# Gaps of 64 and 32 bytes in the pool of slots of a two-block network on one core

## The chip, the core and the metric

The program runs on one core of one Trainium2 chip, batch 1, 256 tokens of 1,024 features. The metric is the device time of one execution in microseconds (us). The kernel before was timed in 2 runs: 2258.93 and 2261.82 us, median 2260.38 us. One more execution was profiled; the rows below are from it.

## What is computed

Two blocks of two layers each, in float32, one behind the other on the same 256 tokens. Nearly all of the arithmetic is products of the tokens with weights that are read once from HBM (the reference, cut):

```python
def first_block(x, ...):                      # layers 0 and 1
    for layer in range(2):
        h = h + 0.5 * _swiglu(_rmsnorm(h, norm_ffn1[layer]), wg, wu, wd)   # 1024 -> 2816 -> 1024
        hn = _rmsnorm(h, norm_mix[layer])
        h = h + (_attn_conv_mixer(hn, ...) if layer == 0 else _recurrent_mixer(hn, ...))
        h = h + 0.5 * _swiglu(_rmsnorm(h, norm_ffn2[layer]), wg, wu, wd)
    return _rmsnorm(h, norm_final)

def second_block(x, c, positions, ...):       # layers 0 and 1
    for layer in range(2):
        sh1, sc1, g1, sh2, sc2, g2 = split(silu(c) @ ada_w[layer] + ada_b[layer], 6)
        x = x + g1 * _mixer(_rms_norm(x, norm_mix) * (1 + sc1) + sh1, ...)   # three kinds of attention
        h = _rms_norm(x, norm_ffn) * (1 + sc2) + sh2
        y = _swiglu_2(h, ...) if layer == 0 else _moe(h, ...)                # 8 experts, 2 per token
        x = x + g2 * y
    return x
```

## The kernel before

**The product in three parts.** TensorE multiplies float32r operands here, which keep fewer bits than float32. So each weight and each activation is split in a high part and a low part. ScalarE (ACT) copies the float32 tile into a float32r tile, the high part; VectorE (DVE) subtracts it from the float32 tile, and the difference is the low part. `mm3` (L329) then makes three matmuls for each 128 features: tokens-high by weights-high (L334), tokens-low by weights-high (L335), tokens-high by weights-low (L337). In the mixture of experts the small experts hold high and low part of 64 tokens side by side in one operand, and two matmuls do (`prod`, L429). In `fmajor` (L595) the roles are exchanged: the weights are loaded into the array and the tokens stream through it.

A matmul has two operands in SBUF. One is loaded into the array ahead of the matmul, 128 columns of 4 bytes from each partition (`lhsT`; the profile shows the load as LDWEIGHTS on the line PEld). The other streams through the array, mostly 512 columns (`rhs`). In `mm3` the tokens are the operand that is loaded and the weights the one that streams. While one matmul streams, the operand of the next is loaded.

**Where the operands lie.** Weights arrive by DMA in 4 buffers `raw` of 8,192 bytes per partition; their high and low parts go to 8 tiles `wh` and 8 tiles `wl` of 4,096 bytes. Everything of the tokens lies in the pool `slots` (L200): 12 places `s0` to `s11`, of 8,192 bytes (`s8` of 4,096), each used for many things in turn. The normed and transposed tokens `xT` are `s0` (high) and `s1` (low), from `new_xT` (L417); the hidden activations of a feed-forward are `s2` and `s3`; a gathered expert's tokens are `s0` or `s1`. Where slots are free for a while, they serve as additional tiles of weights (`ext`, L312): `s9` and `s10` in most feed-forwards, `s2` in the dense one of the second block. Behind the slots stands the pool `cst` (the residual `x`, the identity matrix, constants), and behind it `sm`, the small tiles.

The pools stand one behind the other in the order in which they are opened, and in `slots` a place is given where its tag is first used. In the built program `raw` begins at byte 16,512 of each partition, `wh` at 49,280, `wl` at 82,048, `slots` at 114,816, `x` at 209,024, `ident` at 217,216. Each of these is a multiple of 128, and so is each slice of 128 or 512 columns of them. So before the change, in every one of the 9,076 float32r matmuls that stream 256 columns or more, the operand that is loaded and the one that streams begin at the same place modulo 128. [...]

**Order.** SP issues the loads of weights in the order in which they are used, each as soon as a `raw` buffer is free. The order on each engine is that of the code. Stages: the feed-forwards and mixers of the first block, then those of the second up to about 1430 us, and from there the mixture of experts.

Of the kernel before, what the change touches and what calls it, by code (L numbers as in the profile page):

```python
# [8 lines left out]
F32 = mybir.dt.float32  # L9
F32R = mybir.dt.float32r  # L10
# [182 lines left out]
class K:  # L193
    def __init__(self, ctx, tc, A, out, dbg=None):
        self.tc, self.nc, self.A, self.out, self.dbg = tc, tc.nc, A, out, dbg or {}
        e = ctx.enter_context
        self.raw_p = e(tc.tile_pool(name="raw", bufs=4))
        self.h_p = e(tc.tile_pool(name="wh", bufs=8))
        self.l_p = e(tc.tile_pool(name="wl", bufs=8))
        self.slots = e(tc.tile_pool(name="slots", bufs=1))  # L200
        self.cst = e(tc.tile_pool(name="cst", bufs=1))
        self.sm_p = e(tc.tile_pool(name="sm", bufs=1))
        self.ps = e(tc.tile_pool(name="ps", bufs=4, space=bass.MemoryType.PSUM))
        self.dr = e(tc.tile_pool(name="dr", bufs=1, space=bass.MemoryType.DRAM))
        self.n = 0
        self.ext, self.turn, self.in_moe, self.c_row = (), 0, False, None
        self.first, self.behind = True, None
        self.setup()
# [206 lines left out]
            self.split_T(xT, t, xn, groups=(g,))  # L415

    def new_xT(self):  # L417
        return (self.slot(0, [128, 2, 8, 128], F32R), self.slot(1, [128, 2, 8, 128], F32R))


    def prod(self, out, xs, groups, c0, n, first, last, half=False):
# [972 lines left out]
    def moe(self, h, res, xT, defer):  # L1394
# [21 lines left out]
        def sm(tag, n=16):  # L1416
            return self.small(tag, n, bufs=1).rearrange("p (t e) -> p t e", t=2)
# [78 lines left out]
        def make(got, i, m, half, pcol, gcol):  # L1496

            one, oneT = m[:, 0:256], m[:, 256:512]
            kinds = [(0, half)]
            tables(one, kinds, pcol)  # L1500
            yield
            eT = self.slot(i % 2, [128, 8, 128] if half else [128, 2, 8, 128], F32R)
            got.update(xk=operand(eT, half), half=half, o32=oneT.bitcast(F32))
            yield from gather(one, kinds, [eT], gcol is None)
            got["gs"] = turned(one, oneT, 1, (gcol or (lambda: [gateS[t][:, 0:1] for t in range(2)]))())
# [24 lines left out]
        ct = self.small("ct", 8, bufs=1)  # L1530
# [14 lines left out]
        def by_slot(tag, v, n=8):  # L1545
            r = self.small(tag, 8, bufs=1)
            self.tt(d1, oh, v[:, None, :].to_broadcast([128, 8, 8]), OP.mult)
            nc.vector.tensor_reduce(out=r, in_=d1, axis=AX.X, op=OP.add)
            return r

        eid = by_slot("eid", self.iota8)
# [10 lines left out]
        gateS = [by_slot(f"gateS{t}", gate[:, t]) for t in range(2)]  # L1562

        pov = sm("pov")
        room = self.small("room", 8, bufs=1)
        self.ts(room, place, 1.0, 2.0, OP.is_equal, OP.add)
        self.ts(place, place, 4.5, op0=OP.is_gt)
        self.tt(place, room, place, OP.subtract)
# [14 lines left out]
        def expert(src, got, out, **kw):  # L1583


            def fin(t, acc):
                ye = out()
                for hh in range(2):
                    sl = slice(hh * 512, (hh + 1) * 512)
                    self.stt(ye[:, sl], acc[hh], got["gs"], g2[:, sl], OP.mult, OP.mult)  # L1590

            self.ffn(src, 0, got["xk"], [0], fin, half=got["half"], **kw)
            for _ in scatter([(got["o32"], out())]):
                pass

        def source(s):
            if s == 0:
# [5 lines left out]
        bufs = [self.slot(2, [128, 2, 2, 512], F32R), self.slot(3, [128, 2, 2, 512], F32R), tmp,  # L1603
                {(0, hh): self.mm(512, "acc") for hh in range(2)}]
# [117 lines left out]
        def store():  # L1722
            for t in range(2):
                for hh in range(2):
                    sl = slice(hh * 512, (hh + 1) * 512)
                    (nc.sync if hh == 0 else nc.scalar).dma_start(out=self.out[t * 128:(t + 1) * 128, sl], in_=self.x[t][:, sl])
# [1 line left out]
        store()  # L1728
        flag = nc.values_load(over_i[0:1, 0:1], min_val=0, max_val=256)
        with self.tc.If(flag > 128):  # L1730
            now = self.small("now", 8, bufs=1)
            nc.vector.memset(now, 0.0)
            pc = self.small("pc", 4, bufs=1)
            tmp = sm("ovt")
            hot = self.small("hot", 8, bufs=1)
            with self.tc.For_i(0, 8, 1) as e:
                self.tt(hot, self.iota8, now, OP.is_equal)
                for a, v in ((0, pov), (1, gate)):
                    self.tt(tmp, v, hot[:, None, :].to_broadcast([128, 2, 8]), OP.mult)
                    nc.vector.tensor_reduce(out=pc[:, 2 * a:2 * a + 2], in_=tmp, axis=AX.X, op=OP.add)  # L1740
                self.ts(now, now, 1.0, op0=OP.add)
                src = A["moe"][bass.ds(e, 1)].rearrange("a n -> (a n)")
                m = self.slot(7, [128, 512], F32R)
                got = {}
                for _ in make(got, 0, m, False, [pc[:, t:t + 1] for t in range(2)], lambda: [pc[:, 2 + t:3 + t] for t in range(2)]):
                    pass
                ye = self.slot(10, [128, D])
                expert(src, got, lambda: ye)
            store()
# [122 lines left out]
```

## Time and profile before

| what | value |
|---|---|
| median of 2 runs | 2260.38 us (2258.93 to 2261.82) |
| the profiled execution, its own time | 2259.85 us |
| its span, first to last instruction | 2258.0 us |
| PE busy | 2200.2 us, 97% |
| PEld (loads of the array) busy | 1812.7 us, 80% |
| DVE busy | 1719.0 us, 76% |
| ACT busy | 1336.0 us, 59% |
| mean granted TensorE clock | 0.996 of full speed |

The profiled execution took 1.85 us more than its span and is 0.5 us under the median, so its rows stand for the runs. A matmul's row gives its start and a duration that is modelled: a 512-column matmul is shown with some 390 ns while the next one starts 227 ns after it, since they are pipelined. So PE's busy share tells that it seldom stands still, not how fast it runs; its pace is read from the distance between starts.

### The profile page before, as it was taken

How to read it: one execution, taken by the hardware profiler on the slowest of the kernel's cores; microseconds unless marked ns; L12 is line 12 of the kernel's file. 1: busy time of each engine (PE TensorE's matmuls, PEld its weight loads, DVE VectorE, ACT ScalarE, POOL GpSimd, SP SyncE). 2: the span in 40 equal slices, each digit the busy share in tenths (PEclk: the TensorE clock that was granted, in tenths of full speed). 3: DMA queues.
4: the chain of work that ended last, by engine and by line, in shares of the span. 5: the costliest groups of instructions: out<-in, count | busy, mean ns of one | idle time of the engine just before them, and what ended most of it. 6: DMA issues, size and time to landing. Idle time of an engine off the chain costs nothing.

```text
span 2258.0 us, 29602 instructions
## 1 busy us (share of the span) xinstructions
PE 2200.2 (97%) x10976; PEld 1812.7 (80%) x10976; DVE 1719.0 (76%) x2205; ACT 1336.0 (59%) x1819; POOL 92.9 (4%) x152
## 2 busy tenths in 40 slices
PE   8999999999999999999999999999999999999998
PEld 6888878888888788887888878887788777877777
DVE  6785967658657886675755666889888999889997
ACT  6445554445436744456544475677767776767764
POOL 0001000000000100030000111000000000000000
PEclk9999999999999999999999999999999999999999
DMA  8784258758764587533555442689988888989886
GB/s 339 267 317 163 99 191 318 258 194 311 262 222 159 193 318 264 207 130 131 215 186 183 143 160 108 249 338 336 336 331 326 326 335 320 344 329 347 325 328 242
DMA packets 82263, 572.92 MB, mean 254 GB/s; under 512 B 9373, under 2 KB 9685, under 8 KB 15424
## 3 DMA queue, kind: packets, MB, share of 16 engines
q1 hardware_dynamic: 77616, 556.73, 66.5%
q0 software_dynamic: 3920, 13.12, 1.7%
q8 instruction: 88, 1.44, 0.2%
q10 hardware_dynamic: 576, 1.11, 0.1%
q14 instruction: 63, 0.52, 0.1%
HBM read 569.80 MB, written 1.12 MB: 253 GB/s over the span
## 4 chain that ended last, share of the span: by engine, by line
PE 46%; DVE 5%; ACT 3%; issue 2%; DMA 1%; POOL 1%; ACTq 0%; DVEq 0%; POOLq 0%
PE mm L334 7%; PE mm L335 7%; PE mm L337 7%; PE mm L429 5%; PE acc L335 4%; PE acc L334 4%; PE acc L337 4%; DVE wl L231 3%; PE acc L429 2%; ACT wh L222 2%; PE mm L1579 1%; ACT s L222 1%; DVE s L231 1%; PE mm L595 1%; PE mm L1467 1%
## 5 line engine op out<-in xcount | busy, mean ns | idle before, releaser
L231 DVE TENSOR_TENSOR wl<-raw,wh 128x1024 fp32r<-128x1024 f32 (+1 forms) x908 | 1078.5, 1216 | 272.4 <-ACT wh L222 259.4
L222 ACT ACTIVATE wh<-raw 128x1024 fp32r<-128x1024 f32 (+1 forms) x908 | 921.0, 1052 | 371.4 <-PE mm L335 152.7
L334 PE MATMUL mm<-wh,s 128*128 128x512 f32 (+2 forms) x1384 | 515.9, 378 | 3.2 <-ACT s L222 3.2
L335 PE MATMUL mm<-wh,s 128*128 128x512 f32 (+2 forms) x1384 | 511.1, 374 | 1.0 <-DVE s L231 1.0
L222 ACT ACTIVATE s<-mm 128x512 fp32r<-128x512 f32 (+7 forms) x387 | 200.1, 534 | 346.8 <-PE mm L337 88.3
L337 PE MATMUL mm<-wl,s 128*128 128x512 f32 (+2 forms) x1384 | 396.1, 374 | 0.2
L334 PE MATMUL acc<-wh,s 128*128 128x512 f32 x788 | 312.0, 397 | 4.0 <-ACT s L222 2.1
L335 PE MATMUL acc<-wh,s 128*128 128x512 f32 x788 | 310.5, 394 | 2.2 <-DVE s L231 2.2
L334 PEld LDWEIGHTS mm<-wh,s 128*128 128x128 f32 x1384 | 261.2, 189 | 50.6 <-ACT s L222 4.9
L335 PEld LDWEIGHTS mm<-wh,s 128*128 128x128 f32 x1384 | 261.7, 189 | 47.7 <-DVE s L231 3.3
L337 PEld LDWEIGHTS mm<-wl,s 128*128 128x128 f32 x1384 | 249.5, 189 | 46.4 <-DVE wl L231 1.2
L337 PE MATMUL acc<-wl,s 128*128 128x512 f32 x788 | 251.9, 392 | 0.6 <-DVE wl L231 0.5
L334 PEld LDWEIGHTS acc<-wh,s 128*128 128x128 f32 x788 | 148.6, 189 | 35.5 <-ACT s L222 3.2
L335 PEld LDWEIGHTS acc<-wh,s 128*128 128x128 f32 x788 | 149.0, 189 | 32.4 <-DVE s L231 4.0
L337 PEld LDWEIGHTS acc<-wl,s 128*128 128x128 f32 x788 | 148.1, 189 | 32.5 <-DVE wl L231 2.2
L429 PE MATMUL mm<-wl,s 128*128 128x512 f32 (+1 forms) x384 | 144.1, 382 | 3.2 <-DVE wl L231 3.1
L429 PE MATMUL mm<-wh,s 128*128 128x512 f32 (+1 forms) x384 | 143.3, 381 | 0.0
L231 DVE TENSOR_TENSOR s<-mm,s 128x512 fp32r<-128x512 f32 (+5 forms) x216 | 128.7, 619 | 17.5 <-ACT s L222 16.7
L987 DVE SCALAR_TENSOR_TENSOR raw<-raw,s 128x1024 f32<-128x1024 f32 x96 | 114.2, 1219 | 4.5 <-DMA raw<-in_ada_w 2.6
L231 DVE TENSOR_TENSOR s<-s,mm 128x512 f32<-128x512 f32 (+1 forms) x93 | 59.6, 641 | 46.7 <-PE mm L337 41.1
L222 ACT ACTIVATE s<-raw 128x1024 fp32r<-128x1024 f32 x50 | 52.5, 1061 | 70.8 <-PE mm L337 33.0
L429 PEld LDWEIGHTS mm<-wl,s 128*128 128x128 f32 x384 | 72.5, 189 | 22.5 <-DVE wl L231 9.2
(308 smaller groups left out, 2187.5 us busy)
## 6 DMA issues: line engine op xcount, KB each, us to landing
raw<-in_moe SPq DMA_DIRECT2D x264, 1024.0 KB, 5.6
raw<-in_f SPq DMA_DIRECT2D x132, 1024.0 KB, 5.9
raw<-in_ada_w SPq DMA_DIRECT2D x48, 1024.0 KB, 5.0
raw<-in_dense SPq DMA_DIRECT2D x33, 1024.0 KB, 4.8
raw<-in_w_in SPq DMA_DIRECT2D x12, 1024.0 KB, 4.9
raw<-in_ow_in SPq DMA_DIRECT2D x8, 1024.0 KB, 5.0
raw<-in_w_out SPq DMA_DIRECT2D x8, 1024.0 KB, 6.2
raw<-in_ew_in SPq DMA_DIRECT2D x7, 1024.0 KB, 5.0
```

Source lines behind the costliest of these rows:

```text
L222: return self.nc.scalar.activation(out=out, in_=in_, func=func, **kw)
L231: return self.nc.vector.tensor_tensor(out=out, in0=in0, in1=in1, op=op)
L334: mm(out=out, lhsT=xs[i][0], rhs=ws[i][0], start=first and i == 0, stop=False)
L335: mm(out=out, lhsT=xs[i][1], rhs=ws[i][0], start=False, stop=False)
L337: mm(out=out, lhsT=xs[i][0], rhs=ws[i][1], start=False, stop=last and i == n - 1)
L429: self.nc.tensor.matmul(out=out, lhsT=x[0], rhs=w[j][:, c0:c0 + n], start=first and k == 0 and j == 0, stop=last and k == len(ws) - 1 and ...
L595: mm(out=out, lhsT=a, rhs=b, start=j == 0, stop=j == len(todo) - 1)
L987: self.nc.vector.scalar_tensor_tensor(out=src, in0=src, scalar=1.0, in1=self.c_row, op0=OP.mult, op1=OP.mult, accum_out=p[:, 2 * pc + i:2 ...
L1467: mm(out=p[:, k * w:(k + 1) * w], lhsT=h[t][:, a, kk * 128:(kk + 1) * 128], rhs=one[:, o:o + w], start=t == 0, stop=t == 1)
L1579: mm(out=p, lhsT=o[:, t * 128:(t + 1) * 128], rhs=v[:, sl], start=b == 0, stop=b == len(parts) - 1)
```

## The change

Two tiles that nobody reads or writes are put into the pool of slots: `gap0`, 64 bytes per partition, ahead of all slots, and `gap1`, 32 bytes, behind `s0` and `s1` (taken at the first call of `new_xT` alone, since `first` is true only there). To make room for these 96 bytes, three small tiles of 32 bytes lose tags of their own: `room` now uses the place of `ct`, and, in the part for an overfull expert at the end, `now` that of `ct` and `hot` that of `eid`. That last part is behind a condition and is not entered in the profiled execution.

```diff
@@ -198,6 +198,7 @@
         self.slots = e(tc.tile_pool(name="slots", bufs=1))
+        self.slots.tile([128, 16], F32, tag="gap0", name="gap0")
         self.cst = e(tc.tile_pool(name="cst", bufs=1))
@@ -415,7 +416,10 @@
     def new_xT(self):
-        return (self.slot(0, [128, 2, 8, 128], F32R), self.slot(1, [128, 2, 8, 128], F32R))
+        xT = (self.slot(0, [128, 2, 8, 128], F32R), self.slot(1, [128, 2, 8, 128], F32R))
+        if self.first:
+            self.slots.tile([128, 8], F32, tag="gap1", name="gap1")
+        return xT
@@ -1562,7 +1566,7 @@
-        room = self.small("room", 8, bufs=1)
+        room = self.small("ct", 8, bufs=1)
         self.ts(room, place, 1.0, 2.0, OP.is_equal, OP.add)
@@ -1728,11 +1732,11 @@
-            now = self.small("now", 8, bufs=1)
+            now = self.small("ct", 8, bufs=1)
             nc.vector.memset(now, 0.0)
...
-            hot = self.small("hot", 8, bufs=1)
+            hot = self.small("eid", 8, bufs=1)
```

In the built program of the change the instructions of PE, ACT, POOL and SP are those of before, in the same order, with the same waits; on DVE seven rows name `ct` or `eid` where they named `room`, `now` or `hot`. So nothing is added, removed or moved in time by the program itself. What differs is addresses. Modulo 128 they are:

| tiles | before | change |
|---|---|---|
| `raw`, `wh`, `wl` | 0 | 0 |
| `s8`, `s0`, `s1` (`xT`, gathered tokens) | 0 | 64 |
| `s2` to `s7`, `s9` to `s11` (hidden activations, additional weights, the rest) | 0 | 96 |
| `x`, `ident`, `ones` | 0 | 96 |
| `consts` | 32 | 0 |

## Rows read from the trace of the kernel before

**Rows 1.** Stages: span, busy us (instructions) of PE PEld DVE ACT POOL, clock, DMA, GB/s

```profile
0.00:1430.00 1430.00, 1399.34 (x7172) 1173.67 (x7173) 978.25 (x1388) 741.12 (x1117) 92.30 (x151) 1.00 0.58 213
1430.00:2258.00 828.00, 800.86 (x3805) 639.08 (x3803) 740.73 (x819) 594.85 (x702) 0.64 (x1) 0.99 0.87 325
```

**Rows 2.** The same stages, line L334 alone: PE busy, PEld busy

```profile
0.00:1430.00 1430.00, 646.33 (x1710) 322.21 (x1710) 1.00 0.58 213
1430.00:2258.00 828.00, 262.02 (x686) 129.65 (x686) 0.99 0.87 325
```

**Rows 3.** The second stage, line L429 alone: PE busy, PEld busy

```profile
1430.00:2258.00 828.00, 271.79 (x1120) 197.07 (x1120) 0.99 0.87 325
```

**Rows 4.** The first stage, line L595 alone: PE busy, PEld busy

```profile
0.00:1430.00 1430.00, 94.54 (x768) 93.08 (x768) 1.00 0.58 213
```

**Rows 5.** Timeline of PE, 512 columns: start us, us, engine, line, tiles

```profile
1534.27 0.39 PE L429 MATMUL mm<-wl,s 128*128 128x512 f32 x1
...
1538.81 0.39 PE L429 MATMUL mm<-wl,s 128*128 128x512 f32 x1
...
1539.86 0.39 PE L429 MATMUL mm<-wl,s 128*128 128x512 f32 x1
...
1541.01 0.39 PE L429 MATMUL mm<-wh,s 128*128 128x512 f32 x1
```

**Rows 6.** Timeline of PE, 256 columns

```profile
1310.68 0.64 PE L595 MATMUL mm<-s,wh 128*128 128x256 f32 x4
1311.16 0.40 PE L595 MATMUL mm<-s,wl 128*128 128x256 f32 x2
```

**Rows 7.** Timeline of PE, 512 columns, among the first matmuls of the program

```profile
14.08 0.63 PE L335 MATMUL mm<-wh,s 128*128 128x512 f32 x1
...
15.36 0.71 PE L337 MATMUL mm<-wl,s 128*128 128x512 f32 x2
```

**Rows 8.** Timeline of PE, plain float32, 256 and 128 columns

```profile
272.03 9.67 PE L784 MATMUL acc<-s,s 128*128 128x256 f32 x44
...
47.60 1.03 PE L457 MATMUL mm<-ident,s 128*128 128x128 f32 x8
```

**Rows 9.** Groups of PE by shape: count, busy us, mean ns of one, idle before

```profile
L457 PE MATMUL mm<-ident,s 128*128 128x128 f32 x326 | 46.8, 274 | 0.0
...
L784 PE MATMUL acc<-s,s 128*128 128x256 f32 x62 | 13.9, 380 | 0.0
```

**Rows 10.** Timeline of PE: matmuls around a late load

```profile
2077.19 0.39 PE L429 MATMUL mm<-wl,s 128*128 128x512 f32 x1
2077.41 0.39 PE L429 MATMUL mm<-wh,s 128*128 128x512 f32 x1
2077.64 0.39 PE L429 MATMUL mm<-wl,s 128*128 128x512 f32 x1
...
2114.95 0.40 PE L335 MATMUL acc<-wh,s 128*128 128x512 f32 x1
2115.19 0.62 PE L337 MATMUL acc<-wl,s 128*128 128x512 f32 x2
```

**Rows 11.** Timeline of PEld: the loads in the same places

```profile
2077.19 0.19 PEld L429 LDWEIGHTS mm<-wh,s 128*128 128x128 f32 x1
2077.46 0.19 PEld L429 LDWEIGHTS mm<-wl,s 128*128 128x128 f32 x1
...
2115.00 0.37 PEld L337 LDWEIGHTS acc<-wl,s 128*128 128x128 f32 x2
```

**Rows 12.** Timeline of PE, 416 columns: the first one and the matmul behind them

```profile
962.35 0.35 PE L334 MATMUL mm<-wh,s 128*128 128x416 f32 x1
...
966.87 0.39 PE L334 MATMUL acc<-wh,s 128*128 128x512 f32 x1
```

**Rows 13.** Groups of DVE by shape: count, busy us, mean ns, idle before

```profile
L239 DVE SCALAR_TENSOR_TENSOR s<-s,cols,s 128x256 f32<-128x256 f32 x90 | 39.2, 479 | 0.6
...
L239 DVE SCALAR_TENSOR_TENSOR s<-s,cols,s 128x255 f32<-128x255 f32 x8 | 3.5, 480 | 6.5 <-ACT s L222 6.5
```

## The prediction

> **What bounds the kernel now.** I read the stages first, one up to 1430 us and the mixture of experts behind it. The reader is to see that PE is busy in 1399 of 1430 us and in 801 of 828, at a granted clock of 1.00 and 0.99, the higher of its two levels (2.4 GHz); DVE is next with 68% and 89%, and the DMA moves 213 and 325 GB/s [rows 1]. So the end is set by how fast PE gets through its matmuls: 31 + 27 = 58 us are all that it stands idle.
>
> Next I read PE's pace, from start to start. With 512 columns, 20 matmuls lie between 1534.27 and 1538.81 us: 227.0 ns each [rows 5]. With 256 columns, four lie between 1310.68 and 1311.16: 120 ns [rows 6]. The difference is 107 ns for 256 columns, 0.418 ns per column, one column per cycle at 2.4 GHz. What is left is the same in both: 227 - 214 = 13 ns, 120 - 107 = 13 ns. So each float32r matmul pays 13 ns, some 6% at 512 columns, for something that isn't its columns. This is the only cost that a change of addresses can touch at a size that counts.
>
> Plain float32 pays less. 44 matmuls of 256 columns take 9.67 us [rows 8], the last of which is shown with 0.38 [rows 9]: 9.29/43 = 216 ns. Eight of 128 columns take 1.03, the last with 0.27: 0.76/7 = 109 ns. That is 0.84 ns per column and a rest of 1 to 3 ns. Their operands too begin at 0 modulo 128. And the first matmuls of the program run at half pace: three in 15.36 - 14.08 = 1.28 us, 427 ns for 512 columns [rows 7], 0.834 ns per column, with no rest. So the 13 ns are there only when 4 bytes are read per partition each 0.418 ns. This is what makes a quarrel of two reads, that of the stream and that of the next operand, possible at all.
>
> **The change part by part.** The program adds, removes and moves no instruction, so every term is a change of durations.
>
> *The float32r matmuls.* There are three lines with 1710 in the first stage and 686 in the second [rows 2], 1120 on L429 [rows 3] and 768 on L595 [rows 4]: 3 x 1710 + 768 = 5898, 3 x 686 + 1120 = 3178, together 9076. Nearly all now have 64 (tokens `xT`) or 96 bytes (hidden activations) between their operands modulo 128. From above, each could win 13 - 2 = 11 ns: 9076 x 11 = 100 us. From below nothing, or a loss (below, rivals). I take 0, for two reasons.
>
> First, the two reads don't keep their distance. A plain 128-column matmul needs a load of its own and follows its predecessor in 109 ns [rows 8, 9], so a load of 128 columns, 512 bytes, takes no more. In 109 ns a float32r stream reads 109/0.418 x 4 = 1040 bytes. So the stream gains about 530 bytes on the load, four times 128: whatever they start with, they pass through every distance modulo 128 four times. A start 64 or 96 bytes further moves the moments of meeting, not their number.
>
> Second, the trace has made the trial. A load usually starts with the matmul ahead of it, as at 2077.19 [rows 10, 11]. At 2077.46 one starts 0.05 us late, because what it loads wasn't ready. In 0.05 us the stream has read some 480 bytes (with the rounding of two starts, 380 to 570), so the distance is no longer the one that an equal start gives. The next matmul starts 0.23 us after its predecessor, as ever. At 2115.00 the same happens, and the next starts after 0.24. Without the 13 ns they would show 0.21 or 0.22. And 416-column pieces, every second of which begins 1664 bytes further, an odd multiple of 128, take 4.52/24 = 188.3 ns [rows 12], or 174 and 14: no better.
>
> [...]
>
> *DVE and ACT.* Operands in slots and in `x` begin 64 or 96 bytes further. DVE's taps of 256 columns take 479 ns over 90 starts that differ by 4 bytes from one to the next; those of 255 columns, starting off by 4 bytes in two operands, 480 [rows 13]. Start addresses cost DVE nothing; for ACT I take the same. Bounds: 10 ns, what a row of 480 may hide, on all 819 DVE instructions of the second stage are 8 us, beside 87 us in which DVE idles there [rows 1]; if that cover were gone, 8 us.
>
> *DMA.* The weights go to `raw`, which doesn't move. Loads into slots are issued a stage ahead. Only the first load of `x` and the last store have nothing beside them; the trace shows none that is off 128, and I take 0 (an estimate of mine for the bound is 2 us either way).
>
> *The renamed small tiles.* Same instructions, same engine, same waits: 0. The gaps have no readers.
>
> The sum is made against the profiled execution: 2259.85 + 0 = 2259.85 us, 0.5 under the median of the two runs, so 2260 us.
>
> **The rivals.**
>
> *A, the 13 ns were the equal start.* The half pace speaks for it: the cost comes with the rate of reading [rows 7], and every pair of operands lies at equal places now, so that no row shows a float32r pair 64 or 96 bytes apart from its start. Against it speak the four rounds and the late loads. If it holds, the first stage, PE-bound, wins 5898 x 11 = 65 us. The second would win 35, but must then be fed with 325 x 828/793 = 339 GB/s and have DVE busy in 741 of 793 us [rows 1]; I give it half. 2260 - 82 = 2178 us; if only part of the pairs or of the 13 ns go, up to 2215.
>
> *B, the pairs fall out of step, and it is slower.* The 227 is a state that PE settles into: after the transposes at 1539 us five matmuls take 1541.01 - 1539.86 = 1.15 us, 230 each [rows 5], before the old pace is back, and the one around the late load took 240 [rows 10]. So the meeting of the two reads does have better and worse phases. If the new distance keeps PE from settling, each matmul costs 3 to 13 ns more; at 3 that is 27 us and no more than 2%, from 5.0 ns on (45.2 us/9076) it decides. At 7 ns it is 64 us: 2324. The 416-column pieces, which have a start of their own and pay 14 instead of 13, speak against more than 1 ns, 9 us.
>
> *C, it doesn't do what it says.* Where slots hold weights (`s9`, `s10`) and hidden activations (`s2`, `s3`) at once, both lie at 96, still 0 apart; these are a few hundred of the 9076, so it leaves A at over 90% of its price.
>
> **How the numbers follow.** My forecast, PE's pace within a nanosecond or two of now (the milder part of B is in it), 0.63; A 0.25; B beyond 2% 0.12. About 2% is what a measurement of this kernel can tell from no change, 2215 to 2305 us; so faster 0.25, same 0.63, slower 0.12. The likeliest gives 2260 us. Its own range is 2242 to 2278 (2 ns on 9076 matmuls either way). The whole range goes down to 2180, which leaves out the fuller part of A (some 0.11), and up to 2315, an excess of 6 ns per matmul, which leaves out the worse part of B (some 0.07): 2180 to 2315.
>
> **What would show it.** In the profile of the change, the distance of starts in a run of 512-column matmuls: 227 ns if I am right, 214 to 220 in case A, 230 to 240 in case B; with 256 columns 120, 107 to 112, or more. The first stage should end at 1430 us, within 12; in case A near 1365. DVE's taps should stay at 479 ns. I am wrong if the distance moves by more than 5 ns, and my reasons are wrong if it moves by more than 2. If A comes true in the first stage alone, the second is held by DMA or DVE, and its idle time before PE's matmuls grows.

## The result, and the profile after

The changed kernel takes 2292.57 us (median of 2 runs, 2291.85 and 2293.3) against 2260.38: a ratio of 1.0138 (95% interval 1.0113 to 1.0162), 32 us slower. Less than 2%, but far outside what repeats of one kernel differ by. The forecast was 2260. Its profiled execution took 2293.3 us, its span 2291.5.

First the stages of the changed kernel; the boundary is put where PE has done as many matmuls as at 1430 us before (columns as in [rows 1]: span, busy us and instructions of PE, PEld, DVE, ACT, POOL, clock, DMA, GB/s).

```profile
0.00:1449.00 1449.00, 1419.68 (x7174) 1168.09 (x7175) 978.24 (x1388) 740.70 (x1118) 93.21 (x151) 1.00 0.58 210
1449.00:2291.50 842.50, 815.95 (x3804) 641.37 (x3802) 741.52 (x818) 593.25 (x702) 0.64 (x1) 0.99 0.85 319
```

Beside [rows 1]: the busy times of DVE and ACT and the clock are what they were, and the DMA moves the same bytes in a longer time. PE alone is busier, 1419.7 + 816.0 = 2235.6 against 2200.2 us; the time in which it stands idle is 55.9 us where it was 57.8. So the 33.5 us by which the span grew are PE's own work, done more slowly. A landmark that both programs have shows how they are shared out: the router's matmuls, just ahead of the mixture of experts (line, engine, tiles, count: shortest, median, longest ns, first and last start), before and after:

```profile
L1390 PE MATMUL mm<-rtr,s x32: 170/256/278, 1396.0 to 1418.0; 128*128 128x16 f32 x32
```

```profile
L1394 PE MATMUL mm<-rtr,s x32: 170/256/277, 1415.6 to 1438.0; 128*128 128x16 f32 x32
```

The last of them starts 20.0 us later, and 13.5 us are lost behind it.

The pace answers [rows 5]: matmuls of 512 columns on the same line (L429 before, L433 now; start, us, engine, line, tiles).

```profile
1552.84 0.39 PE L433 MATMUL mm<-wh,s 128*128 128x512 f32 x1
...
1559.14 0.40 PE L433 MATMUL mm<-wl,s 128*128 128x512 f32 x1
```

27 distances in 6.30 us are 233.3 ns each, where there were 227.0. And with 256 columns, against [rows 6]:

```profile
1326.41 0.63 PE L599 MATMUL mm<-s,wh 128*128 128x256 f32 x4
...
1330.65 0.63 PE L599 MATMUL mm<-s,wh 128*128 128x256 f32 x4
```

36 matmuls in 4.24 us, 117.8 ns, where there were 120: these became *faster*. The trace also holds pairs that the change left 0 apart: where `s9` or `s10` hold weights and `s2`, `s3` the hidden activations, all are at 96. Twelve matmuls lie between the first and the last of these rows:

```profile
67.37 0.39 PE L335 MATMUL acc<-s,s 128*128 128x512 f32 x1
...
70.09 0.39 PE L335 MATMUL acc<-s,s 128*128 128x512 f32 x1
```

2.72 us, 226.7 ns: the old pace, in the middle of the changed kernel. Averaged over the float32r matmuls of the trace that follow back to back and whose operands now lie apart, 512 columns went from 227.4 to 233.5 ns and 256 columns from 119.9 to 116.2. Of 7,292 matmuls with 512 columns all but 216 lie apart now, so 7,076 x 6.1 - 1,688 x 3.7 = 43 - 6 = 37 us. PE's busy time grew by 35.4, and about 2 us less idle time leave 33.5 of span.

DVE and ACT are untouched, as [rows 13] would have it: DVE's taps take 483 ns where they took 479, with 39.2 us in all both times. The taps, and the two instructions that split the weights (in both kernels 1219 and 1054 ns):

```profile
L240 DVE SCALAR_TENSOR_TENSOR s<-s,cols,s 128x256 f32<-128x256 f32 x90 | 39.2, 483 | 0.6
...
L232 DVE TENSOR_TENSOR wl<-raw,wh 128x1024 fp32r<-128x1024 f32 x896 | 1066.2, 1219 | 281.7 <-ACT wh L223 277.9 <-PE mm L336 0.3 <-PE mm L599 0.3
L223 ACT ACTIVATE wh<-raw 128x1024 fp32r<-128x1024 f32 x896 | 909.4, 1054 | 364.2 <-PE mm L336 156.8 <-PE acc L336 129.3 <-DMA raw<-in_moe 19.3
```

So the place of the loss is plain. What the experiments had to tell: is it the *difference* of the two start addresses, the address itself, or something else that the gaps moved; modulo what; and what the 13 ns are that matmuls paid before.

### The profile page after: what moved, and what is told of

The parts are those of the page before. It is cut to its first block, busy times and chain, and to the rows that moved or that the text cites. A ratio compares the mean times of both kernels' runs of the same rounds, so it can differ in the third digit from the quotient of the medians.

```text
span 2291.5 us, 29602 instructions
## 1 busy us (share of the span) xinstructions
PE 2235.6 (98%) x10976; PEld 1809.5 (79%) x10976; DVE 1719.8 (75%) x2205; ACT 1333.9 (58%) x1819; POOL 93.9 (4%) x152
## 4 chain that ended last, share of the span: by engine, by line
PE 49%; DVE 4%; ACT 2%; issue 1%; POOL 1%; DMA 0%; DVEq 0%; ACTq 0%; POOLq 0%
PE mm L335 7%; PE mm L336 7%; PE mm L338 7%; PE mm L433 6%; PE acc L336 4%; PE acc L338 4%; PE acc L335 4%; PE acc L433 3%; DVE wl L232 3%; PE mm L1583 1%; ACT wh L223 1%; PE mm L1471 1%; DVE s L232 1%; PE mm L599 1%; PE mm L680 1%
## 5 line engine op out<-in xcount | busy, mean ns | idle before, releaser
L338 PE MATMUL mm<-wl,s 128*128 128x512 f32 (+2 forms) x1384 | 401.7, 377 | 0.5 <-DVE wl L232 0.5
L335 PE MATMUL acc<-wh,s 128*128 128x512 f32 x788 | 315.6, 402 | 3.5 <-DVE s L232 1.7
L336 PE MATMUL acc<-wh,s 128*128 128x512 f32 x788 | 314.0, 399 | 2.4 <-DVE s L232 2.4
L433 PE MATMUL mm<-wl,s 128*128 128x512 f32 (+1 forms) x384 | 146.3, 388 | 2.9 <-DVE wl L232 2.7
L433 PE MATMUL mm<-wh,s 128*128 128x512 f32 (+1 forms) x384 | 146.4, 389 | 0.0
L991 DVE SCALAR_TENSOR_TENSOR raw<-raw,s 128x1024 f32<-128x1024 f32 x96 | 114.2, 1219 | 3.1 <-ACT s L223 1.7
L433 PEld LDWEIGHTS mm<-wl,s 128*128 128x128 f32 x384 | 73.5, 191 | 23.3 <-DVE wl L232 8.7
```

The costliest lines, as they stand in the source:

```text
L335: mm(out=out, lhsT=xs[i][0], rhs=ws[i][0], start=first and i == 0, stop=False)
L336: mm(out=out, lhsT=xs[i][1], rhs=ws[i][0], start=False, stop=False)
L338: mm(out=out, lhsT=xs[i][0], rhs=ws[i][1], start=False, stop=last and i == n - 1)
L433: self.nc.tensor.matmul(out=out, lhsT=x[0], rhs=w[j][:, c0:c0 + n], start=first and k == 0 and j == 0, stop=last and k == len(ws) - 1 and ...
L991: self.nc.vector.scalar_tensor_tensor(out=src, in0=src, scalar=1.0, in1=self.c_row, op0=OP.mult, op1=OP.mult, accum_out=p[:, 2 * pc + i:2 ...
```

## The experiments

### Which address counts: m1, e1, e2

m1 runs nothing but matmuls of ready operands. Its core, cut (the tiles `W`, streamed, and `L`, loaded, begin equal modulo 256):

```python
def run(name, n, s, l):            # stream begins s bytes into W, the load l bytes into L
    for i in range(48):
        nc.tensor.matmul(out=p, lhsT=L[:, l // 4:l // 4 + 128], rhs=W[:, s // 4:s // 4 + n], ...)
```

> Leaves the whole computation out: it only runs 48 float32r matmuls in a row for each of some 40 pairs of start addresses, all loads and streams ready, and copies x to the output. Theory T1 (the pace hangs on the difference of the two start addresses modulo 128): 512 columns at difference 0 take 227 ns, at 64 and 96 about 233, at 128 and at 256 to 4096 again 227; stream and load both at 64 take 227, stream at 64 with load at 0 some 233; 256 columns 120 ns at 0, 116 at 64, 117.5 at 96. Theory T2 (an operand that begins off a multiple of 128 is itself slower): both at 64 take 233 or more. Theory T3 (addresses do nothing to PE here, the time went through DVE, ACT or the small tiles): 227 and 120 at every difference.

The rows of its timeline: each is one setting (the number is the load's offset in bytes, both_ has both at 64), and its us run to the end of the last of 48, which is shown with 0.39 us (0.28 with 256 columns). So (us - 0.39) / 47 is the pace.

```profile
53.76 11.36 PE L42 MATMUL dsixtyfour__273<-w,l 128*128 128x512 f32 x48
...
76.08 11.40 PE L42 MATMUL dninetysix__371<-w,l 128*128 128x512 f32 x48
...
98.52 11.37 PE L42 MATMUL donetwentyeight__469<-w,l 128*128 128x512 f32 x48
...
142.99 5.93 PE L42 MATMUL dzero__665<-w,l 128*128 128x256 f32 x48
...
165.84 5.61 PE L42 MATMUL dsixtyfour__861<-w,l 128*128 128x256 f32 x48
...
210.97 11.05 PE L42 MATMUL dtwofiftysix__1253<-w,l 128*128 128x512 f32 x48
...
265.38 11.08 PE L42 MATMUL both__1498<-w,l 128*128 128x512 f32 x48
```

64: 233.4 ns. 96: 234.3. Both at 64: 227.4, the first ten still settling. 256: 226.8. So far T1. But 128 bytes give 233.6: the offsets repeat after 256, not after 128. And the sign counts: with the stream at 64 and the load at 0, which is 192 modulo 256, 512 columns took 229 ns where T1 had 233. From here on an offset says how far the load begins behind the stream, modulo 256. With 256 columns 64 bytes give 113.4 against 120.2. Plain float32 took 215.8 ns for 256 columns at 0 and at 64.

e1 and e2 put the same question to the kernel.

```diff
 e1                                                 e2
-gap0, gap1 (slots at 0 again)                     -gap0, gap1
+self.cst.tile([128, 24], F32, tag="gap")          +self.raw_p.tile([128, 16], F32, tag="gap", bufs=1)
 (x, ident, constants, small tiles 96 further)      (raw, wh, wl, slots, x all 64 further)
```

> The slots stand at 0 modulo 128 again, only the pools behind them (x, the identity, constants, small tiles) are moved by 96 bytes, and the three renamed small tiles keep their new names. T1 and T2 (the operands of the float32r matmuls): as the kernel before, 2260 us within 4, 512 columns at 227 ns. T3 (the moved constants, x, small tiles and renames cost the time, through DVE, ACT or DMA): 2292 us.

> Everything, raw buffers, high and low parts of the weights, slots, x, is moved by 64 bytes together, so that load and stream begin equal modulo 128 again, but each off a multiple of 128. T1 (the difference): 2260 us within 5, 227 ns for 512 columns and 120 for 256. T2 (the absolute place of the loaded operand): some 2290 us, 233 ns.

e1: 2258.58 us, ratio 0.9994 (0.9984 to 1.0004). e2: 2259.96 us, 0.9995 (0.9984 to 1.0007). Both as the kernel before: neither the moved constants, the residual and the renamed tiles (T3) nor an operand off a multiple of 128 (T2) cost anything. It is the difference between load and stream that counts.

### The size of the step, and part of the change alone: m2, e3, e4, e5

> Leaves the whole computation out: 48 float32r matmuls in a row for each pair of start addresses (the loaded operand 0 to 248 bytes behind the streamed one, in steps of 8, with 512 and with 256 columns), and x copied to the output. The first micro run gave 226.7 ns at 0, 16 and 256, but 233.3 at 128. Theory P (the differences repeat after 256 bytes, not after 128): 512 columns stay near 233 at 128 and come down only towards 240 to 256; the far_ pieces (128 apart, either way) take 231 to 234, back_ (0) and equal_ (both at 128) 226.7. Theory H (the pace is inherited from the piece before, and 128 was slow only because 112 ran ahead of it): far_ behind a piece at 0 stays at 227. Cold_ (64 apart, half clock) should pay no rest: 427 ns.

m2 went through 0 to 248 bytes in steps of 8. With 512 columns nothing is below 226.7 ns; most offsets stand at 230 to 234. But 120 bytes settled at 226.7 as well, so an equal start is not the only one with that pace. In the first 5 us of the run, where matmuls go at half pace, 64 bytes apart took 427 ns, with no rest, as expected. Offsets 0 and 128 in turn:

```profile
569.33 11.32 PE L42 MATMUL far__3311<-w,l 128*128 128x512 f32 x48
580.49 11.05 PE L42 MATMUL back__3360<-w,l 128*128 128x512 f32 x48
591.37 11.35 PE L42 MATMUL far__3409<-w,l 128*128 128x512 f32 x48
```

far_, 128 bytes apart, takes 232.6 and 233.2, back_, 0 apart, 226.8 between them: theory P. So H is wrong for 128. Yet some offsets have two settled paces: 16 bytes took 226.8 ns in m1, behind the setting at 0, and 233.4 here, behind 8. With 256 columns, 64 bytes settled at 113.3 in m1 and m2 but at 117.8 in m3. That the setting ahead decides it fits H, but no run shows it apart. 0 came down to 226.7 each time, after up to ten matmuls (235, 234, 235, 225, 230, 236, 229, 232, 231, 227, then 226.7).

```diff
-        self.slots.tile([128, 16], F32, tag="gap0", name="gap0")      # the change: 16 words, and gap1
+        self.slots.tile([128, 32], F32, tag="gap0", name="gap0")      # e3, no gap1
+        self.slots.tile([128, 4], F32, tag="gap0", name="gap0")       # e4, no gap1
                                                                       # e5: gap1 alone
```

> One gap of 128 bytes ahead of the slots and none behind s1, so that all the tokens' operands begin equal to the weights modulo 128 but 128 apart modulo 256; the renamed small tiles stay, and one more small tile shares a tag to make the room. If the offsets count modulo 256, as the first micro run says: 512 columns at 233 ns, 256 at 118.5; about 7,100 x 5.9 - 1,650 x 1.5 = +39 us, some 2299 us. If they count modulo 128, as the change puts it: 227 and 120 ns, 2260 us.

> One gap of 16 bytes ahead of the slots and none behind s1, the renamed small tiles kept: hardly any pair of operands begins equal any more. If the settled pace of the first micro run carries over (226.7 ns at 16 as at 0, and 120 with 256 columns): 2260 us within 5. If only an equal start gives the old pace: 512 columns at 230 ns or more, from 2280 us up.

> The gap of 64 bytes ahead of the slots is left out, that of 32 behind s1 stays: pairs with s0, s1 or s8 and weights begin equal again (4,032 of 512 columns), those with s2 to s7 and s9 to s11 32 bytes apart (3,260). By the pace per pair (233.2 against 227.3 ns at 32 bytes): 3,260 x 5.9 - 250 x 1.6 = +19 us, 2279 us, the pairs with hidden activations at 233 and those with xT at 227 ns. If the whole layout of the pool mattered and not the pair: 227 or 233 for all of them, 2260 or 2290 us.

e3: 2289.45 us, ratio 1.0132 (1.0115 to 1.0148), 512 columns at 232.6 ns where they lie 128 apart: equal modulo 128 and nearly as slow as the change. It is 10 us less than forecast. 528 of the 7,292 pairs have both operands in slots and stayed equal, and the pace of the others is 0.7 ns below that of m1. e4: 2288.29 us, 1.0135 (1.0115 to 1.0155). Here the edit missed its aim: the pool rounds 16 bytes up to 32, as its addresses show, and 32 apart is what it measured, 233.2 ns; whether 16 bytes would keep the pace in the kernel wasn't tried. e5: 2276.28 us, 1.0056 (1.004 to 1.0073): pairs with `xT` back at 227.6 ns, pairs of hidden activations and weights at 233.2. 16.6 us in the profiled span for 19 expected. The loss is that of each pair by itself, and it adds up.

### Can the 256 columns win alone: e6

The main lines of the edit, cut (`xT` of two mixers is moved by 64 bytes too):

```diff
-        per = max(1, 1024 // n)
+        at = 16 if n == 256 and move else 0        # weights of 256 columns 64 bytes into their tiles
+        per = 3 if at else max(1, 1024 // n)
+            h, l = h[:, at:], l[:, at:]
```

> No gaps; instead only the pairs with 256 columns are put 64 bytes apart, where the micro runs gave 113.3 ns against 120: weights in pieces of 256 columns are written 64 bytes into their tiles (three chunks per tile, not four), and xT of the two mixers of the first block 64 bytes into its slot. 1,472 of 1,688 pairs with 256 columns are 64 apart then, and 48 with 512 columns too. By the pace per pair: -1472 x 6.5 + 48 x 6 = -9 us, 2251 us, if the added piece of work per eight chunks on ACT and DVE stays hidden; if DVE's or ACT's added work shows in the second stage, 2255 to 2262.

2260.91 us, ratio 1.0001 (0.9985 to 1.0016): no gain. The stages:

```profile
0.00:1430.00 1430.00, 1394.01 (x7165) 1166.82 (x7166) 975.93 (x1391) 741.58 (x1126) 95.06 (x151) 1.00 0.59 212
1430.00:2259.00 829.00, 799.46 (x3813) 638.19 (x3811) 743.30 (x841) 597.53 (x719) 0.64 (x1) 1.00 0.87 325
```

PE's busy time fell from 2200.2 to 2193.5 us, less than forecast because the pairs ran at 116.8 ns and not at 113.4. The forecast took the price of the wrong offset. In m1's setting of 64 bytes the load begins further on; here the operand that streams does, which is 192 modulo 256. At 192 m2 took 117.9 ns (m1, with its stream at 64, 113.2):

```profile
513.21 5.82 PE L42 MATMUL qdzero__2870<-w,l 128*128 128x256 f32 x48
```

PE's idle time rose from 57.8 to 65.8; the added pieces of weights are the likely reason, which no run shows apart. The two cancel.

### What the 13 ns are: m3, m4, m5

> Leaves the whole computation out: 48 float32r matmuls in a row per setting, and x copied to the output. The settings vary the load: 128, 96, 64 or 32 columns wide, 0 or 64 bytes behind the stream, with 512 and 256 columns streaming; then bfloat16 operands, a stream that takes its columns with a stride, a load with a stride of 8 bytes, and a stream with a skip of 64 to 192 bytes in its middle. Theory S (what a matmul pays beyond its columns is the reading of the next load, 128 columns for 13.3 ns at distance 0): 96, 64 and 32 columns pay 10, 6.7 and 3.3 ns, so 223, 220 and 217 ns with 512 columns, and the 64-byte penalty shrinks with them. Theory G (a fixed gap between matmuls): 227 and 120 ns whatever the load's width. bfloat16, which reads half the bytes: no more than 217 and the same at all distances by S, as plain float32 showed.

Settings of m3: full, half and quarter are loads of 128, 64 and 32 columns at 0 bytes; comb is a stream that takes its columns in turn from the two halves of the 512, 0, 256, 1, 257 and so on (`W[:, 0:512].rearrange("p (a b) -> p b a", a=2)`), here at 64 bytes.

```profile
20.14 11.04 PE L48 MATMUL fullzero__130<-w,l 128*128 128x512 f32 x48
...
86.84 11.20 PE L48 MATMUL halfzero__522<-w,l 128*64 128x512 f32 x48
...
119.94 11.28 PE L48 MATMUL quarterzero__718<-w,l 128*32 128x512 f32 x48
...
153.07 10.54 PE L48 MATMUL bfzero__914<-wb,lb 128*128 128x512 bf16 x47
...
225.85 10.52 PE L48 MATMUL combtwosixtyfour__1355<-w,l 128*128 128x512 f32 x48
```

226.6, 230.0 and 231.7 ns: with 512 columns less to load made it *slower*, against theories S and G. With 256 columns it made it faster: 120 ns with the full load at 0, 113.4 with 64 columns and with 32. bfloat16 takes 216 ns at every offset. And the comb, in the same float32r, takes 215.8, at an offset that costs a contiguous stream 233. Taking the columns in turn from four or sixteen places instead of two is slow: 283 and 434 ns. A load with a stride of 8 bytes (233 and 230 ns at 0 and 64 bytes) and a skip in the middle of the stream (230 to 233) win nothing.

> Leaves the whole computation out: 48 float32r matmuls in a row per setting, and x copied to the output. The third micro run gave 215.8 ns for 512 columns when the stream takes them in turn from two halves that lie 1,024 bytes apart, at 0 and at 64 bytes of offset. Theory S (the rest is the quarrel between stream and load): such a stream runs at 216 to 218 ns at every offset (0, 8, 32, 64, 96, 128, 192), 416 columns at 176 and 256 at 109; when it takes 2, 4 or more columns from a half before it changes over, the rest comes back, towards 227. If the gain belongs to the one distance of 1,024 bytes: 256 columns (512 bytes apart) and the settings with 1,040 to 2,048 bytes stay at 227 and 120.

m4 confirmed the comb: 215.8 ns at 0, 8, 32, 64, 96, 128 and 192 bytes, 175.8 with 416 columns, 111.7 with 256, for halves 1,024 to 2,048 bytes apart (4,096 with 256 columns). Two, four or eight columns from a half before it changes over:

```profile
71.69 10.52 PE L42 MATMUL infar__371<-w,l 128*128 128x512 f32 x48
...
241.49 16.17 PE L42 MATMUL blocktwo__1400<-w,l 128*128 128x512 f32 x48
257.49 12.17 PE L42 MATMUL blockfour__1449<-w,l 128*128 128x512 f32 x48
```

are worse than no comb (333, 250, 243 ns), not merely back at 227. Whether the rest belongs to the load or to the stream, m5 asked.

> Leaves the whole computation out: 48 float32r matmuls in a row per setting, and x copied to the output. Loads of 1, 2, 8, 16, 32 and 64 columns at 0 and 64 bytes, with 512 and 256 columns streaming; the stream in turn from two halves with loads of 1 and 32 columns; operands of 64 and 32 partitions; a stream with a step of 8 or 16 bytes, one that reads two places over and over, and one that takes its columns in turn from pieces 32, 64 and 128 bytes apart. Theory S (the rest is what the stream loses to the reading of the load): with one column to load 512 columns take 216 ns, at both offsets. Theory O (the rest is the contiguous stream's own, and the load's place only moves it a little): with one column still 227 to 233 ns, and 216 only where the order of the stream is changed. The third run (230 ns with 64, 232 with 32 columns to load) speaks for O.

```profile
19.61 11.26 PE L48 MATMUL monezero__130<-w,l 128*1 128x512 f32 x48
30.70 11.26 PE L48 MATMUL monesixtyfour__179<-w,l 128*1 128x512 f32 x48
...
218.67 10.52 PE L48 MATMUL combone__1306<-w,l 128*1 128x512 f32 x48
...
356.68 10.52 PE L48 MATMUL closeeight__1747<-w,l 128*128 128x512 f32 x48
```

With one column to load, 512 columns take 231.3 ns at 0 and at 64 bytes alike: theory O. At half pace 512 columns took 427 ns (m2); half of that, 213.5 ns, stands here as an estimate of the columns alone, and 107 for 256. With next to nothing to load the contiguous float32r stream takes some 18 ns more, and loads of up to 32 columns leave it there. With 256 columns the same small loads leave 7 to 10 ns (113.3 to 116.7 ns), so this loss grows with the columns. A load of 128 columns changes it by its place: with 512 columns down to 13 ns where both begin equal modulo 256, up to 20 at most other places. The comb has no such loss, even with pieces only 32 bytes apart (closeeight). Two words read over and over take 219 ns. The settings with 32 partitions can't be read, since the granted clock fell there (0.81 in the mean of the 100 us around, below). A stream with a step of 8 or 16 bytes can, since the clock was back at 1.00 (the stretch below the rows):

```profile
307.39 16.87 PE L48 MATMUL steptwo__1600<-w,l 128*128 128x512 f32 x37
324.08 21.34 PE L48 MATMUL stepfour__1649<-w,l 128*128 128x512 f32 x46
```

```profile
308.00:324.00 16.00, 16.00 (x37) 7.30 (x36) 0.00 (x0) 0.00 (x0) 0.00 (x0) 1.00 0.00 0
```

37 distances in 16.69 us are 451 ns for 512 columns, twice the contiguous pace, and a step of 16 bytes takes 460. So a stride alone doesn't make a stream fast; taking the columns one by one in turn from two places does.

### Does it hold in the kernel: e7, e8, then e9, e10

e7 is the kernel before with the comb. So that the output keeps its order, the weights are written into their tiles in the inverse order; ACT and DVE then read `raw` with a stride of 8 bytes. e8 is the same on the changed kernel. Of the edit, cut:

```diff
+                    u = min(n, 512)            # even columns to the first half, odd ones to the second
+                    hv, lv, r = self.comb(hv, u)[0], self.comb(lv, u)[0], self.comb(r, u)[1]
+                self.act(hv, r, AF.Copy)
+        return v.rearrange("p (a b) -> p b a", a=2) if self.mix else v      # the stream
```

> The kernel before, with the weights that stream written into their tiles in another order: of each 512 columns (or 416, 256) the even ones in the first half, the odd ones in the second; the matmul takes them in turn from the two halves, so its output is in the old order. ACT and DVE read the raw weights with a stride of 8 bytes for that. Nothing is added or moved in memory; the 768 matmuls of the fmajor line and a few others stay as they were. Theory S (13 ns are the quarrel between stream and load, which this stream avoids): 512 columns at 216 to 218 ns, some 8,200 matmuls x 11 = 90 us for PE, of which the first stage shows 55 and the second, with DVE and DMA near their limits, half of 35: 2187 us. If the strided reading makes ACT and DVE slower by a tenth or more, the second stage gives its part back: 2205 to 2260. If the gain needs the same operands each time: 2260.

> The same order of columns, put on the changed kernel with both gaps. Theory S: without the quarrel there is nothing that an offset could make worse, so as e7 within 8 us (the fmajor line has 117 instead of 120 ns, -2 us). If the offset works by another way than the reading of both operands: 30 us above e7.

e7: 2305.92 us, ratio 1.0199 (1.0181 to 1.0217). e8: 2301.42, 1.0179 (1.0161 to 1.0197). Slower, and the profile of e7 shows why:

```profile
1430.00:2305.00 875.00, 788.65 (x3707) 627.32 (x3705) 825.60 (x774) 772.02 (x689) 0.00 (x0) 0.97 0.82 303
```

```profile
L244 DVE TENSOR_TENSOR wl<-raw,wh 128x1024 fp32r<-128x1024 f32 x896 | 1253.0, 1440 | 167.2 <-ACT wh L235 164.7 <-PE mm L355 0.9 <-PE acc L357 0.2
L235 ACT ACTIVATE wh<-raw 128x1024 fp32r<-128x1024 f32 x896 | 1245.9, 1467 | 212.4 <-PE mm L355 75.9 <-PE acc L355 63.5 <-DMA raw<-in_f 38.9
```

The stride made a DVE piece 18% and an ACT piece 39% longer (1440 for 1219, 1467 for 1054 ns), and in the mixture of experts DVE is now busy in 826 of 875 us and PE in 789: DVE, with ACT ahead of it, is now the busiest engine instead of PE. The router's last matmul (1400.6 us) starts 17.4 us earlier than before, though; 64 us are lost behind it. (The access pattern of these reads is longer too, and no run takes the two apart.) That e8 is not above e7 spoke for the theory, but with PE off the path it proves little.

e9 leaves the weights in order and lets the output come out in the comb's order. The hidden activations keep it until their transposes load them with a stride; the residual sums read PSUM with it. e10 is e9 on the changed kernel. Of the edit, cut:

```diff
+        cut = lambda v: v[:, c0:c0 + n].rearrange("p (a b) -> p b a", a=2)
-        self.mm3(out, ..., [(h[:, c0:c0 + n], l[:, c0:c0 + n]) for h, l in g], ...)
+        self.mm3(out, ..., [(cut(h), cut(l)) for h, l in g], ...)
-   transpose(p[:, k * 128:(k + 1) * 128], u[:, k * 128:(k + 1) * 128], ident)
+   transpose(p[:, k * 128:(k + 1) * 128], self.block(u, n, k), ident)       # stride of 8 bytes
-        self.stt(xs, acc[h], 0.5, xs, OP.mult, OP.add)
+        self.stt(self.flat(xs), self.back(acc[h]), 0.5, self.flat(xs), OP.mult, OP.add)
```

> The kernel before, with the weights in their tiles as they were; the stream of some 7,000 matmuls with 512 columns and 850 with 256 takes its columns in turn from the two halves, so their output columns stand in that order in PSUM, and those who read them put it right: the transposes of the hidden activations and the first gather load with a stride of 8 bytes, the residual sums read PSUM with it. ACT and DVE read the raw weights as ever. Theory S (the rest beyond the columns is the quarrel of stream and load, and it is on the path): 216 ns for 512 columns, 112 for 256: 7,000 x 11.5 + 850 x 8.2 = 87 us less PE time; the first stage shows its 55, the second, where DVE is busy in 741 of 828 us, half of 32: 2190 us, between 2172 and 2215. If the stride where PSUM is read, or the loads of the transposes, cost more than they do in the micro runs: 2215 to 2260.

> The same stream order on the changed kernel, with both gaps. Theory S: the change's offsets have nothing to work on in the 7,850 matmuls that take columns in turn, and only the fmajor line (768, 117 against 120 ns) and some 290 others with 512 columns (233 against 227) still feel them: within 3 us of e9. If the change's 33 us come by another way (loads, stores, other engines): 30 us above e9.

e9: **2191.52 us, ratio 0.9713 (0.9692 to 0.9734)**, 2.9% faster than the kernel before. e10: 2194.43 us, ratio 0.9713 (0.9697 to 0.973): where the gaps cost 32 us before, the medians now differ by 2.9, less than the runs of either kernel among themselves. e9 came out as forecast (2190), but theory S, by which it was forecast, is the one that m5 speaks against: e9 shows that the comb's pace holds in the kernel, not where the rest comes from. Stages and pace of e9:

```profile
0.00:1384.00 1384.00, 1348.63 (x7173) 1177.18 (x7174) 974.90 (x1388) 737.73 (x1117) 93.38 (x151) 1.00 0.61 220
1384.00:2188.90 804.90, 773.83 (x3804) 648.63 (x3802) 739.91 (x819) 595.12 (x702) 0.64 (x1) 0.99 0.89 334
```

```profile
1479.18 0.38 PE L439 MATMUL mm<-wl,s 128*128 128x512 f32 x1
...
1489.11 0.38 PE L439 MATMUL mm<-wl,s 128*128 128x512 f32 x1
```

46 distances in 9.93 us: 215.9 ns. DVE and ACT have their old durations (1219 and 1051 ns a piece) and busy times. PE's busy time is 2122.5 against 2200.2 us; its idle time rose from 57.8 to 66.4, so 69 of 78 us reach the end. By the router's landmark 44.7 of them fall in the first stage and 24.4 in the second, where DVE is busy in 740 of 805 us and PE in 774.

## Why the prediction was wrong, point by point

**Right: PE bounds the kernel, and what addresses can touch is its pace.** All of the loss is in PE's busy time; ACT, DVE, DMA and the renamed tiles were rightly put at 0 (e1, with `x` 96 bytes further: 2258.58 us, ratio 0.9994). The prediction's sums stand on 0.418 ns per column, from [rows 5] and [rows 6]; its 2.4 GHz is 1/0.418 ns, and the profile gives the clock as a share of full speed alone. The time lies within the outer range, 2180 to 2315, but that is the width of the range: the likeliest part, 2242 to 2278, missed it, and the distance of starts moved by 6.3 ns where "more than 5" was named as the sign of being wrong.

**Wrong, the step that decided: "A start 64 or 96 bytes further moves the moments of meeting, not their number."** On this step the sum put the 9,076 matmuls at 0. It took the rest for a number of meetings of two reads that stays the same wherever they begin. The runs show that it does not: the settled pace hangs on where the load begins, with a period of 256 bytes, 226.7 ns at 0 and 233.3 at 64, and in the kernel this term was 37 us. Nor does the rest come from meetings alone, or stand apart from the columns ("something that isn't its columns"): with one column to load m5 still has 18 ns with 512 columns, and 10 with 256.

**Wrong: "the trace has made the trial"** with a late load at 2077.46 us [rows 11]. One shifted matmul among settled ones doesn't show the pace of a shifted run: m2 takes up to ten matmuls to settle. The load was late for another reason than the prediction gives, too: the tokens that it loads were there, and it waited for `wl`, which its matmul streams and which DVE finished at 2077.41. The 0.24 us at 2115.00 [rows 10] and the five matmuls of 230 ns [rows 5], which count for rival B alone in the prediction, look like the settling that m2 shows, though no run tests that.

**Wrong size: rival B.** Its mark ("230 to 240 in case B") came true, 233, and so did its point, that the new distance is slower. But PE is not kept from settling; it settles at a slower pace (at 64 bytes 231 and 236 ns in turn, m1). It was priced at no more than 1 ns, 9 us, by the 416-column pieces, which start at other places [rows 12]. Such pieces were the wrong witness: at 0, 64 and 128 bytes 416 columns take 188.3, 186.7 and 190.0 ns in the micro runs, so they hardly tell the offsets apart (in the changed kernel, where their starts alternate, they went from 188.8 to 193.5). The term measured 6.1 ns on 7,076 matmuls, 43 us, and -3.7 ns on 1,688 with 256 columns, -6 us, which rival B did not have. Its sum fell short of the 45.2 us from which, in the prediction's words, "it decides".

**Wrong: rival A as put.** An equal start was not the cause of the 13 ns. Of the 32 offsets of m2 none gave 512 columns less than the 226.7 ns of an equal start. The 256 columns alone gain by an offset, and in the kernel (e6) the little that PE gained was lost again as idle time (PE busy 6.7 us less, idle 8.0 us more). Of the 100 us that the prediction put at most for the 13 ns, e9 won 68, by the order of the stream and not by an offset.

**Right: rival C's pairs.** They kept 226.7 ns, and so show within the one trace that it is the pair that counts.

**What stays open.** Why a contiguous float32r stream of 512 columns loses 18 ns and a comb 2 to 3; why a full load 0 apart eases it with 512 columns and not with 256; why 120 bytes are as good as 0, and why 16 bytes settled at two different paces. The runs show that it is so, and not what in the memory does it.

## What to carry to other kernels

Read the distance between matmul starts against the columns at the granted clock (0.418 ns each in [rows 5] and [rows 6]): what is left over is a cost of its own, and a few lines of matmuls on ready operands, with one thing changed at a time, tell more of it than reasoning from single rows. For float32r with 512 columns, take the streamed columns one by one in turn from two halves (216 instead of 227 ns here; a plain step of 8 bytes gave 451, four places 283), and put the order right where few bytes are read, in PSUM and in transposes (e9, 2191.52 us), not in the instructions that carry the weights (e7, 2305.92). If a stream of 512 columns must stay contiguous, let load and stream begin equal modulo 256 (226.7 ns here against 233.3 at 64 bytes; with 256 columns that was no better than other offsets, 120 ns), and don't shift pools by a few words without measuring the pace again.

## What the runs showed of the hardware that was not expected

- Less to load is not always faster: 512 columns took 226.6 ns beside loads of 128 columns 0 apart, 231.7 beside 32, 231.3 beside one. With 256 columns it is: 120 beside 128, 113.4 beside 32.
- The comb's grain matters: one column in turn 215.8 ns, two 333, four 250, eight 243, sixteen 240, thirty-two 237. Two places, not more: four 283, sixteen 434. A plain step of 8 bytes 451.
- Reading with a stride of 8 bytes, in e7's access pattern, cost ACT more (39%) than DVE (18%) for pieces of 1,024 float32.
- In m5, after 22 us of matmuls that used 64 of the 128 partitions and 1 us of matmuls that used 32, the granted clock fell for 44 us (512 columns at 427 ns, where they had taken 230 and 233 with 64 partitions; 0.81 in the mean of the 100 us around), with PE busy without a break. The two stretches, without and with it:

```profile
100.00:200.00 100.00, 100.00 (x580) 59.05 (x579) 0.00 (x0) 0.00 (x0) 0.00 (x0) 1.00 0.00 1
200.00:300.00 100.00, 100.00 (x415) 71.15 (x414) 0.00 (x0) 0.00 (x0) 0.00 (x0) 0.81 0.00 1
```
